# Heads of the two expert stages of a decoder trunk: routing tables on GpSimd, first rows split ahead of the tables, two matrices split beside attention's end

## The chip, the core and the metric

The kernel runs on one core of one Trainium2 chip. The core has five engines with queues of their own: TensorE (PE in the profile; PEld is its weight load), VectorE (DVE), ScalarE (ACT), GpSimd (POOL) and SyncE (SP, which only issues transfers here). The metric is the device time of one launch in microseconds. Lower is better.

## What is computed

A trunk of two layers over 512 tokens of width 1024. Layer 0 mixes tokens with RWKV-7, layer 1 with forgetting attention. After each mixer comes a LayerNorm and a mixture of 16 experts, whose router is shared: the best of four groups, and in it the best two experts.

```python
h = layer_norm(ALPHA * h + mixed, ln_g[i, 0], ln_b[i, 0])
ffn = shared_router_moe(h, router_w, router_bias, ...)
h = layer_norm(ALPHA * h + ffn, ln_g[i, 1], ln_b[i, 1])
...
s = jax.nn.sigmoid(xt @ router_w); s_sel = s + router_bias
grp_score = jnp.sum(lax.top_k(s_sel, 2)[0], -1); g_star = jnp.argmax(grp_score, -1)
_, loc = lax.top_k(in_grp, TOP_K); e_idx = g_star[:, None] * EXPERTS_PER_GROUP + loc
gate = jnp.take_along_axis(s, e_idx, axis=1); gate = gate / jnp.sum(gate, -1, keepdims=True)
...
hid = jax.nn.silu(xb @ w_gate[e]) * (xb @ w_up[e]); ys = hid @ w_down[e]
out = jax.ops.segment_sum(ys * row_gate[:, None], row_tok, num_segments=n_tok + 1)[:n_tok]
```

## The kernel before

All tokens stand in four tiles of 128. Every fp32 product is made of three: both operands are split into a high part (`wh`, `xm`, `xh`; ACT copies to fp32r, line 200 for weights, line 64 for rows) and a low part (the difference, on VectorE, lines 203 and 65), and high by high, low by high and high by low are summed.

An expert's weights are six matrices of 1 MB (`place`): two of gate, two of up, two of down. They go through a ring of eight landing tiles `raw`, numbered m = 0, 1, 2, ... over all experts. `wsplitA(m)` makes the high part on ACT, `wsplitB(m)` the low part on VectorE and then issues the load of matrix m+8 on SP. Six high and six low tiles exist.

`moe` is one expert stage and is called for both layers. Its **head** comes before the loop over experts. On VectorE it picks group and experts (lines 209 to 231, ending in the 0/1 table `selb`), on PE it counts positions, and then it finds the rows of the first expert: `first(0)` makes the list of 128 token rows and gathers them into `xg` (line 253, an indirect transfer on POOL), `gather2(0)` gathers the half rows of the next 64 tokens (second block) into `xo` (line 262), and `first(1)` does the same as `first(0)` for expert 1. What follows on VectorE, in this order: the low part of matrix 0 (`loA(0)`); the routing tables (lines 391 to 408: position and block of each token, the two choices of each token as masks `m1` and `mk`, sums over experts `red`, the index `idx` and the gate `rec`); the gates of expert 0 in three bf16 pieces `gp` (lines 411 to 414); then, after the eight scatters of the tables on POOL have been issued (line 423), the low parts of the gathered rows `xm`, of matrix 1, of the second block's rows `xh`, and of matrices 2 to 5.

The loop over experts begins with `more(0)`, the second block of expert 0, which is run if it has over 128 tokens, as it does in both layers here. On PE that is: products with matrices 0 and 1 (16 of 512 columns), twelve small ones with `gp` that give the block's gates (`gates0(1)`, line 419), products with matrices 2 and 3 (32 of 256 columns), transposes, and products with 4 and 5. PE takes them in this order:

```python
guB(w[0],0); guB(w[1],1); nc.scalar.activation(xo,pgo,AF.Copy)
if e==0: gates0(1)
guB(w[2],2); upB(0,f2)
guB(w[3],3); upB(1,f2); hidBT(0); hidBS(0); hidBT(1); hidBS(1)
```

The work inside `moe` is issued as written. The attention stage `fox` is ordered by `Threads`, a planner in which each strand says what it needs and how long it holds an engine; its last strands are `t_oproj` (output projection, residual sum at line 1254), `t_last` (LayerNorm, `ln_steps`: statistics on VectorE, root and normalisation on ACT, scale and shift as four VectorE operations, line 148) and `t_route` (transposes, router product, sigmoid).

Of the kernel before, what the change touches and what calls it, by code (L numbers as in the profile page):

```python
# [176 lines left out]

def moe(C, L, W, hd, zd, load, tail, late=()):

# [4 lines left out]
    with ExitStack() as ctx:  # L184
# [205 lines left out]
        bl=su[:,256:320].rearrange("p (a b) -> p a b",b=NE); code=su[:,320:384].rearrange("p (a b) -> p a b",b=NE); pos=pp[:,0:NT,:]  # L390
        V.tensor_scalar(bl,pos,127.5,None,op0=ALU.is_gt)
        for n in (255.5,383.5): V.scalar_tensor_tensor(bl,pos,n,bl,op0=ALU.is_gt,op1=ALU.add)
        V.scalar_tensor_tensor(code,pos,64.0,C.e4[:,None,:].to_broadcast([128,NT,NE]),op0=ALU.mult,op1=ALU.add)
        V.scalar_tensor_tensor(code,bl,-8191.0,code,op0=ALU.mult,op1=ALU.add)
        mk=su[:,384:512].rearrange("p (c t e) -> p c t e",c=2,e=NE); m1=mk[:,1].rearrange("p t (g e) -> p (t g) e",g=4)
        V.memset(m1[:,:,0],0.0); V.tensor_copy(m1[:,:,1],selv[:,:,0])
        V.tensor_tensor(m1[:,:,2],selv[:,:,0],selv[:,:,1],op=ALU.add)
        V.tensor_tensor(m1[:,:,3],m1[:,:,2],selv[:,:,2],op=ALU.add)
        V.tensor_tensor(mk[:,1],mk[:,1],sel,op=ALU.mult)
        V.tensor_tensor(mk[:,0],sel,mk[:,1],op=ALU.subtract)  # L400
        mt=sTs[0].rearrange("p a b -> p (a b)").rearrange("p (c t e) -> p c t e",c=2,e=NE); red=p1.tile([128,3,8],F32,name="red"); idx=p1.tile([128,8],I32,name="idx")
        ct=lambda t: t.rearrange("p c t e -> p (c t) e"); bc=lambda t: t[:,None,:,:].to_broadcast([128,2,NT,NE])
        V.tensor_tensor(mt,mk,bc(code),op=ALU.mult)
        V.tensor_reduce(red[:,0,:,None],ct(mt),axis=AX.X,op=ALU.add); V.tensor_copy(idx,red[:,0])
        V.tensor_tensor(mt,mk,bc(s),op=ALU.mult)
        V.tensor_reduce(red[:,1,:,None],ct(mt),axis=AX.X,op=ALU.add)
        V.tensor_tensor(red[:,2,0:4],red[:,1,0:4],red[:,1,4:8],op=ALU.add); V.reciprocal(red[:,2,0:4],red[:,2,0:4]); V.tensor_scalar(red[:,2,0:4],red[:,2,0:4],1.0/ALPHA,None,op0=ALU.mult)
# [953 lines left out]
```

## Time and profile before

| | us |
|---|---|
| median of 3 runs | 1638.11 (1634.1 to 1641.88) |
| profiled execution, own time | 1635.95 |
| its span in the trace | 1634.2 |

| engine | busy us | share |
|---|---|---|
| PE | 1459.5 | 89% |
| PEld | 1192.7 | 73% |
| DVE | 1163.1 | 71% |
| ACT | 919.5 | 56% |
| POOL | 530.7 | 32% |

The span is the stretch between the trace's first and last record; 1.75 us of the execution's own time lie outside it. A timeline row gives start, duration, engine, line, operation, output and inputs with their shapes, and in brackets how long the engine had been idle and what released it. The granted clock is 1.00 where TensorE runs at 2.4 GHz and 0.50 where it runs at 1.2 GHz.

### The profile page before, as it was taken

Reading aid. Unit: us, or ns where it says so; the run is one execution under the profiler, and the core shown is the slowest. Engines: PE = TensorE matmul, PEld = TensorE weight load, DVE = VectorE, ACT = ScalarE, POOL = GpSimd, SP = SyncE. Lnnn points to the kernel's source line nnn. Section 1 sums busy time; section 2 is a strip of 40 time slices with the busy share of each in tenths; the row PEclk is TensorE's granted clock in tenths of the full one; section 3 lists DMA queues with packets and bytes.
Section 4 is the critical chain, followed back from the end, with each engine's and each line's share of the span. In section 5 each row is a group of like instructions: output and inputs, shape, how many; then the busy total and the mean of one; then the engine's idle time right before and its main releaser. Section 6 shows DMA issues by size and latency. Waiting matters only on the chain. (4 is left out here: it accounts for less than half of the span.)

```text
span 1634.2 us, 24892 instructions
## 1 busy us (share of the span) xinstructions
PE 1459.5 (89%) x9125; PEld 1192.7 (73%) x9125; DVE 1163.1 (71%) x1873; ACT 919.5 (56%) x1355; POOL 530.7 (32%) x431
## 2 busy tenths in 40 slices
PE   6998977889976799999999699999885999999992
PEld 2587865887765688888887577777674888888881
DVE  7647779477585796887895637556647786968984
ACT  2553573534334486767885436545424786858872
POOL 4104785413242433322342323101104233313422
PEclk9998998587987899999999799999995999999996
DMA  7325532133345799897992424112427797979962
GB/s 221 123 84 187 162 99 83 27 98 117 111 142 189 239 331 316 287 358 232 357 344 94 157 72 123 37 61 72 155 104 227 244 364 247 358 249 346 350 204 106
DMA packets 202521, 313.61 MB, mean 192 GB/s; under 512 B 27914, under 2 KB 123490, under 8 KB 202356
## 3 DMA queue, kind: packets, MB, share of 16 engines
q1 hardware_dynamic: 178820, 267.74, 48.1%
q0 software_dynamic: 18816, 37.31, 8.0%
q10 hardware_dynamic: 4720, 6.44, 1.1%
q8 instruction: 93, 1.52, 0.4%
q14 instruction: 72, 0.59, 0.1%
HBM read 296.42 MB, written 41.75 MB: 207 GB/s over the span
## 5 line engine op out<-in xcount | busy, mean ns | idle before, releaser
L203 DVE TENSOR_TENSOR wl<-raw,wh 128x2048 fp32r<-128x2048 f32 (+1 forms) x168 | 334.7, 2006 | 5.9 <-DVEq L344 5.9
L200 ACT ACTIVATE wh<-raw 128x2048 fp32r<-128x2048 f32 (+1 forms) x168 | 282.7, 1688 | 15.7 <-ACT wh L200 9.0
L339 POOL DMA_INDIRECT zd<-yt,TB x38 | 113.7, 2992 | 432.2 <-ACT yt L306 386.0
L68 PE MATMUL bank<-wh,xm 128*128 128x256 f32 (+1 forms) x768 | 249.9, 325 | 3.9
L69 PE MATMUL bank<-wl,xm 128*128 128x256 f32 (+1 forms) x768 | 245.1, 319 | 0.0
L70 PE MATMUL bank<-wh,xm 128*128 128x256 f32 (+1 forms) x768 | 244.9, 319 | 0.0
L68 PEld LDWEIGHTS bank<-wh,xm 128*128 128x128 f32 x768 | 144.6, 188 | 26.0 <-issue 14.6
L69 PEld LDWEIGHTS bank<-wl,xm 128*128 128x128 f32 x768 | 144.7, 188 | 11.5
L70 PEld LDWEIGHTS bank<-wh,xm 128*128 128x128 f32 x768 | 144.6, 188 | 11.3
L203 DVE TENSOR_TENSOR wl<-rawo,wh 128x2048 fp32r<-128x2048 f32 (+1 forms) x56 | 110.2, 1980 | 24.9 <-ACT wh L200 24.4
L68 PE MATMUL bank<-wh,wh 128*128 128x512 f32 x256 | 111.5, 436 | 1.4 <-DVE kl L1169 0.8
L68 PE MATMUL bank<-wh,hm 128*128 128x512 f32 x256 | 111.3, 435 | 0.0
L70 PE MATMUL bank<-wh,wl 128*128 128x512 f32 x256 | 101.1, 395 | 3.6 <-DVE wl L1240 3.6
L70 PE MATMUL bank<-wh,hm 128*128 128x512 f32 x256 | 101.1, 395 | 0.0
L69 PE MATMUL bank<-wl,hm 128*128 128x512 f32 x256 | 100.8, 394 | 0.0
L200 ACT ACTIVATE wh<-rawo 128x2048 fp32r<-128x2048 f32 (+1 forms) x56 | 93.4, 1668 | 13.1 <-PE bank L70 9.0
L69 PE MATMUL bank<-wl,wh 128*128 128x512 f32 x256 | 100.6, 393 | 0.0
L1062 POOL TENSOR_TENSOR wl<-raw,wh 128x512 fp32r<-128x512 f32 x29 | 41.2, 1432 | 88.6 <-ACT wh L1061 87.0
L262 POOL DMA_INDIRECT xo<-hd,TB x30 | 61.1, 2037 | 11.9 <-issue 8.6
L64 ACT ACTIVATE xm<-bank 128x512 fp32r<-128x512 f32 x64 | 38.3, 598 | 42.5 <-PE bank L280 38.9
L68 PEld LDWEIGHTS bank<-wh,wh 128*128 128x128 f32 x256 | 49.2, 192 | 15.1 <-issue 6.0
L1197 ACT ACTIVATE sb<-sb,st 128x512 f32<-128x512 f32 (+1 forms) x64 | 35.8, 560 | 43.2 <-DVE st L1193 27.3
(531 smaller groups left out, 3504.1 us busy)
## 6 DMA issues: line engine op xcount, KB each, us to landing
raw<-in_moe_w_gate_dram SPq DMA_DIRECT2D x48, 1024.0 KB
raw<-in_moe_w_up_dram SPq DMA_DIRECT2D x48, 1024.0 KB
raw<-in_moe_w_down_dram SPq DMA_DIRECT2D x48, 1024.0 KB
rawo<-in_moe_w_up_dram SPq DMA_DIRECT2D x16, 1024.0 KB
rawo<-in_moe_w_down_dram SPq DMA_DIRECT2D x16, 1024.0 KB
rawo<-in_moe_w_gate_dram SPq DMA_DIRECT2D x14, 1024.0 KB
raw<-in_fx_w_in_dram SPq DMA_DIRECT2D x12, 1024.0 KB
raw<-in_rw_wk_dram SPq DMA_DIRECT2D x4, 1024.0 KB
```

Source lines behind the costliest of these rows:

```text
L64: nc.scalar.activation(hi,src,AF.Copy)
L68: nc.tensor.matmul(out,ah,bh,start=start,stop=False)
L69: nc.tensor.matmul(out,ah,bl,start=False,stop=False)
L70: nc.tensor.matmul(out,al,bh,start=False,stop=stop)
L200: Q=slice(None) if q is None else QS[q]; nc.scalar.activation(his[m%NH][:,Q],raws[m%NR][:,Q],AF.Copy)
L203: Q=slice(None) if q is None else QS[q]; V.tensor_tensor(los[m%NH][:,Q],raws[m%NR][:,Q],his[m%NH][:,Q].bitcast(F32),op=ALU.subtract)
L262: nc.gpsimd.indirect_dma_start(out=xo,out_offset=None,in_=hd.rearrange("t (h n) -> (t h) n",h=2), in_offset=bass.IndirectOffsetOnAxis(ap=T ...
L339: nc.gpsimd.indirect_dma_start(out=zd[:,:],out_offset=bass.IndirectOffsetOnAxis(ap=ix[0:n],axis=0), in_=y[0:n],in_offset=None,bounds_check ...
L1062: (V if d else G).tensor_tensor(lo[n][:,Q],raw[:,Q],hi[n][:,Q].bitcast(F32),op=ALU.subtract)
L1197: S.activation(SB[u][:,0:N],SB[u][:,0:N],AF.Exp,bias=ST[u][:,0:1],scale=-1.0,accum_out=ST[u][:,1:2])
```

## The change

In both heads, `mk` (the masks of first and second choice) is made from a second threshold `thr1`, by one VectorE comparison and two POOL operations ahead of the first gather. The sums over experts are no longer VectorE reductions; `total` halves the 16 experts in four additions on POOL. The sum for the gates is issued on POOL between `first(0)` and `gather2(0)`, that for the index after the gathers. The VectorE part of the tables shrinks to five small operations and two on `red`. The splitting of the gathered rows and of matrices 1 to 5 is written ahead of the rest of the tables, and the gates `gr`, `gp` of expert 0 come behind the low part of matrix 5.

In layer 1 alone (`pre=2`), the high and low parts of matrices 0 and 1 are made in `fox`, on ACT and VectorE, by a new strand `t_early` and at the end of the last `t_last`; their successors, matrices 8 and 9, are then loaded at the head's start. The last tile's LayerNorm there is `ln_quick`: statistics by halves, and subtraction with scale, then multiplication with shift, as two VectorE operations for each half, with no ACT normalisation.

```diff
+def ln_quick(C, th, z, i, gb, bb, mark, eps=LN_EPS, keys=()):
+    V=C.nc.vector; sm=C.sm[:,i%4]; N=(slice(0,512),slice(512,1024))
+    for n in range(2):
+        yield from th.need(*keys[n:n+1])
+        V.bn_stats(sm[:,6*n:6*n+6],z[:,N[n]]); yield 'V',.69
+    V.bn_aggr(sm[:,12:14],sm[:,0:12].rearrange("p (a b) -> p a b",a=2))
+    V.tensor_scalar(sm[:,14:15],sm[:,13:14],eps,None,op0=ALU.add)
+    C.nc.scalar.activation(sm[:,15:16],sm[:,14:15],AF.Sqrt)
+    sub=lambda n: V.scalar_tensor_tensor(z[:,N[n]],z[:,N[n]],sm[:,12:13],gb[:,N[n]],op0=ALU.subtract,op1=ALU.mult)
+    sub(0); V.reciprocal(sm[:,14:15],sm[:,15:16]); yield 'V',1.2
+    for n in range(2):
+        if n: sub(1)
+        V.scalar_tensor_tensor(z[:,N[n]],z[:,N[n]],sm[:,14:15],bb[:,N[n]],op0=ALU.mult,op1=ALU.add); yield 'V',.69*(n+1)
+        mark(n)
...
-        for m in range(NH): wsplitA(m)
+        for m in range(pre,NH): wsplitA(m)
...
+        V.tensor_tensor(m0,rk,C.thr1[:,None,:].to_broadcast([128,16,4]),op=ALU.is_lt)
+        G.tensor_tensor(m0,m0,gs.rearrange("p t g -> p (t g)")[:,:,None].to_broadcast([128,16,4]),op=ALU.mult)
+        G.tensor_tensor(mk[:,1],selb,mk[:,0],op=ALU.subtract)
...
         first(0)
...
+            for n in (8,4,2): G.tensor_tensor(t[:,:,0:n],t[:,:,0:n],t[:,:,n:2*n],op=ALU.add)
+            G.tensor_tensor(out,t[:,:,0],t[:,:,1],op=ALU.add)
+        G.tensor_tensor(mt2,mk,bc(s),op=ALU.mult); total(red[:,1],mt2)
+        G.tensor_tensor(red[:,2,0:4],red[:,1,0:4],red[:,1,4:8],op=ALU.add)
...
-        loA(0); V.tensor_copy(sel,selb)
+        V.reciprocal(red[:,2,0:4],red[:,2,0:4]); V.tensor_scalar(red[:,2,0:4],red[:,2,0:4],1.0/ALPHA,None,op0=ALU.mult)
+        for m in range(pre): load(m+NR)
...
+        if not pre: loA(0)
+        for hf in range(2): xposeT(xgs[0],hf,tr[hf]); xposeS(hf,tr[hf])
+        if not pre: loA(1)
+        xposeB()
+        for m in range(2,NH): loA(m)
+        G.tensor_tensor(mt,mk,bc(code),op=ALU.mult); total(red[:,0],mt)
+        G.tensor_copy(idx,red[:,0])
...
         V.tensor_tensor(gr,s[:,:,ORDER[0]],red[:,2,0:4],op=ALU.mult)
...
-        for hf in range(2): xposeT(xgs[0],hf,tr[hf]); xposeS(hf,tr[hf])
-        loA(1); xposeB()
-        for m in range(2,NH): loA(m)
...
     def t_last(i):
-        yield from need(f"r{i}0",f"r{i}1")
-        yield from after.norm(i,z[i],th,z[i])
+        if i<NT-1: yield from need(f"r{i}0",f"r{i}1")
+        yield from after.norm(i,z[i],th,z[i],(f"r{i}0",f"r{i}1"))
+        if i==NT-1: after.lo(0,1); after.lo(1)
+    def t_early():
+        yield from need(f"r{NT-1}0")
+        yield .8
+        after.hi(0,0); yield 'S',.95
+        after.lo(0,0); yield 'v',1.15
+        after.hi(0,1); after.hi(1); yield 'S',2.9
...
-        moe(C,1,W,hd[1],zd[1],load[1],0)
+        moe(C,1,W,hd[1],zd[1],load[1],0,pre=2)
```

VectorE's queue in the head of layer 0, before (`gp` are expert 0's gates, `xm` and `xh` the gathered rows, `wl` a matrix's low part):

```order
L411 TENSOR_TENSOR gr<-s,red 128x4
L413 CAST gp<-gr 128x4
L414 TENSOR_TENSOR gr<-gr,gp 128x4
L413 CAST gp<-gr 128x4
L414 TENSOR_TENSOR gr<-gr,gp 128x4
L413 CAST gp<-gr 128x4
L65 TENSOR_TENSOR xm<-bank_3958,xm 128x512
L65 TENSOR_TENSOR xm<-bank_3959,xm 128x512
L203 TENSOR_TENSOR wl_3944<-raw_62,wh_3938 128x2048
L65 TENSOR_TENSOR xh<-bank_3958,xh 128x256 x2
L203 TENSOR_TENSOR wl_3945<-raw_63,wh_3939 128x2048
L203 TENSOR_TENSOR wl_3946<-raw_64,wh_3940 128x2048
```

The same place now, from the low part of matrix 0 on; three more rows of `gr` and `gp` follow the last one:

```order
L219 TENSOR_TENSOR wl_3945<-raw_61,wh_3939 128x2048
L65 TENSOR_TENSOR xm<-bank_3960,xm 128x512
L65 TENSOR_TENSOR xm<-bank_3961,xm 128x512
L219 TENSOR_TENSOR wl_3946<-raw_62,wh_3940 128x2048
L65 TENSOR_TENSOR xh<-bank_3960,xh 128x256 x2
L219 TENSOR_TENSOR wl_3947<-raw_63,wh_3941 128x2048
L219 TENSOR_TENSOR wl_3948<-raw_64,wh_3942 128x2048
L219 TENSOR_TENSOR wl_3949<-raw_65,wh_3943 128x2048
L219 TENSOR_TENSOR wl_3950<-raw_66,wh_3944 128x2048
L437 TENSOR_TENSOR gr<-s,red 128x4
L439 CAST gp<-gr 128x4
L440 TENSOR_TENSOR gr<-gr,gp 128x4
```

The six operations of the gates stood ahead of the rows and are now behind the low parts of matrices 2 to 5 (`wl` from `raw_63` to `raw_66`). PE's queue has kept its order.

POOL's queue in the head of layer 1, before, from the first gather on:

```order
L253 DMA xg_17915<-hd_136,i_17974 128x1024
L262 DMA xo<-hd_136,i_18008 128x512
L253 DMA xg_17916<-hd_136,i_17974 128x1024
L269 TENSOR_LOAD cnt x2
L423 DMA tab_17908<-rec,idx 8192x4 x8
L427 DMA TB<-tab_17908 128x256
L429 DMA TB_17910<-tab_17908 128x1x256
L430 TENSOR_SCALAR TB_17910<-TB_17910,odd 128x64
```

And now:

```order
L274 DMA xg_17922<-hd_138,i_17982 128x1024
L286 TENSOR_TENSOR sT_17921<-su,s 128x128
L284 TENSOR_TENSOR sT_17921<-sT_17921 128x8x8
L284 TENSOR_TENSOR sT_17921<-sT_17921 128x8x4
L284 TENSOR_TENSOR sT_17921<-sT_17921 128x8x2
L285 TENSOR_TENSOR red<-sT_17921 128x8
L287 TENSOR_TENSOR red<-red 128x4
L293 DMA xo<-hd_138,i_18024 128x512
L274 DMA xg_17923<-hd_138,i_17982 128x1024
L300 TENSOR_LOAD cnt x2
L432 TENSOR_TENSOR sT_17920<-su 128x128
L284 TENSOR_TENSOR sT_17920<-sT_17920 128x8x8
```

Six operations for the gates' sum stand between the first gather and that of the second block, and seven for the index (two are shown) ahead of the scatters.

VectorE's queue at the end of attention, before, from the last tile's two residual sums on:

```order
L1254 SCALAR_TENSOR_TENSOR raw_66<-raw_66,bank_3956 128x512
L1254 SCALAR_TENSOR_TENSOR raw_66<-raw_66,bank_3957 128x512
L123 BN_STATS sm<-raw_66 128x6 x2
L124 BN_AGGR sm<-sm 128x2
L125 TENSOR_SCALAR sm<-sm 128x1
L130 RECIPROCAL sm<-sm 128x1
L131 SCALAR_TENSOR_TENSOR sm<-sm 128x1
L148 TENSOR_TENSOR raw_66<-raw_66,raw_63 128x512 x4
L209 TENSOR_TENSOR su<-s,rbt 128x64
```

And now:

```order
L1277 SCALAR_TENSOR_TENSOR raw_66<-raw_66,bank_3958 128x512
L157 BN_STATS sm<-raw_66 128x6
L1337 TENSOR_TENSOR wl_3945<-raw_61,wh_3939 128x1024
L1277 SCALAR_TENSOR_TENSOR raw_66<-raw_66,bank_3959 128x512
L157 BN_STATS sm<-raw_66 128x6
L158 BN_AGGR sm<-sm 128x2
L159 TENSOR_SCALAR sm<-sm 128x1
L161 SCALAR_TENSOR_TENSOR raw_66<-raw_66,sm,raw_63 128x512
L162 RECIPROCAL sm<-sm 128x1
L165 SCALAR_TENSOR_TENSOR raw_66<-raw_66,sm,raw_63 128x512
L161 SCALAR_TENSOR_TENSOR raw_66<-raw_66,sm,raw_63 128x512
L165 SCALAR_TENSOR_TENSOR raw_66<-raw_66,sm,raw_63 128x512
```

One half of a low part of matrix 0 stands between the two residual sums, and the four operations behind the statistics are fused ones.

## Rows read from the trace of the kernel before

**Rows 1.** table by stretch, layer 0 experts: busy by engine, clock, DMA share
```profile
580.00:604.00 24.00, 23.85 (x143) 20.66 (x142) 21.89 (x18) 19.70 (x20) 11.31 (x6) 1.00 1.02 339
```

**Rows 2.** timeline of DVE, layer 0 head: start us, us, line, operation, tiles
```profile
530.54 2.29 DVE L203 TENSOR_TENSOR wl<-raw,wh 128x2048 fp32r<-128x2048 f32 x1
...
537.02 0.15 DVE L411 TENSOR_TENSOR gr<-s,red 128x4 f32<-128x4 f32 x1
...
538.01 0.40 DVE L413 CAST gp<-gr 128x4 bf16<-128x4 f32 x1
...
538.09 1.28 DVE L65 TENSOR_TENSOR xm<-bank,xm 128x512 fp32r<-128x512 f32 x2
...
539.29 2.28 DVE L203 TENSOR_TENSOR wl<-raw,wh 128x2048 fp32r<-128x2048 f32 x1
...
541.49 0.41 DVE L65 TENSOR_TENSOR xh<-bank,xh 128x256 fp32r<-128x256 f32 x1
...
542.71 8.95 DVE L203 TENSOR_TENSOR wl<-raw,wh 128x2048 fp32r<-128x2048 f32 x4
```

**Rows 3.** timeline of PE, layer 0 head, up to hidden rows
```profile
534.15 1.97 PE L280 MATMUL bank<-ident,xg 128*128 128x128 f32 x8 [5.64 <-DMA xg<-hd,i]
...
542.01 0.77 PE L314 MATMUL bank<-wh,xh 128*128 128x512 f32 x1 [2.06 <-issue]
...
547.71 0.45 PE L419 MATMUL bank<-gp,yt 128*128 128x1 bf16 x12
...
548.02 0.37 PE L314 MATMUL bank<-wh,xh 128*128 128x256 f32 x1
...
551.90 0.55 PE L326 MATMUL bank<-pair,xo 128*128 128x64 f32 x4
```

**Rows 4.** timeline of ACT, layer 0 head: the second copy of gathered rows
```profile
536.16 0.60 ACT L64 ACTIVATE xm<-bank 128x512 fp32r<-128x512 f32 x1 [0.20 <-PE bank L280]
```

**Rows 5.** timeline of POOL, layer 0: issue of the first gather
```profile
527.08 1.10 POOL L253 DMA_INDIRECT xg<-hd,i  x1 [4.35 <-issue]
```

**Rows 6.** timeline of DVE, layer 1: LayerNorm of the last tile
```profile
1221.09 1.28 DVE L123 BATCH_NORM_STATS2 sm<-raw 128x6 f32<-128x512 f32 x2
...
1224.31 2.75 DVE L148 TENSOR_TENSOR raw<-raw,raw 128x512 f32<-128x512 f32 x4 [0.88 <-ACT raw L135]
```

**Rows 7.** timeline of PE, layer 1 head
```profile
1225.78 1.11 PE L154 MATMUL bank<-ident,raw 128*128 128x128 f32 x4 [5.33 <-DVE raw L148]
...
1243.67 1.94 PE L280 MATMUL bank<-ident,xg 128*128 128x128 f32 x8 [3.10 <-DMA xo<-hd,i]
...
1253.71 0.76 PE L314 MATMUL bank<-wh,xh 128*128 128x512 f32 x1 [2.11 <-DVE xh L65]
...
1260.17 0.45 PE L419 MATMUL bank<-gp,yt 128*128 128x1 bf16 x12
```

**Rows 8.** timeline of POOL, layer 1: issue of the first two gathers
```profile
1239.10 1.07 POOL L253 DMA_INDIRECT xg<-hd,i  x1 [4.34 <-issue]
1240.48 1.05 POOL L262 DMA_INDIRECT xo<-hd,i  x1 [0.30 <-DVE sg L248]
```

**Rows 9.** costliest groups, the smallest form of POOL: busy us, mean ns
```profile
L717 POOL COPY Lam<-Ep 128x8 f32<-128x8 f32 x8 | 3.6, 445 | 0.5
```

**Rows 10.** timeline of PE, a gap in the RWKV mixer
```profile
477.75 1.11 PE L919 MATMUL rb<-ident,y 128*128 128x128 f32 x4 [5.36 <-DVE y L917]
```

**Rows 11.** table by stretch around that gap and in the layer 1 head
```profile
474.00:476.00 2.00, 0.00 (x0) 0.00 (x0) 2.00 (x3) 0.00 (x0) 1.27 (x1) 0.63 0.00 0
482.00:484.00 2.00, 1.58 (x16) 1.49 (x13) 1.47 (x4) 1.62 (x4) 0.42 (x1) 1.00 0.57 174
1254.00:1258.00 4.00, 4.00 (x10) 3.13 (x10) 3.97 (x3) 0.00 (x1) 3.08 (x4) 0.50 0.95 271
1260.00:1264.00 4.00, 4.00 (x43) 3.83 (x42) 3.88 (x4) 1.88 (x2) 3.61 (x2) 1.00 1.01 393
```

**Rows 12.** timeline of DVE: a LayerNorm addition beside a POOL subtraction
```profile
487.76 1.65 DVE L148 TENSOR_TENSOR res<-res,raw 128x512 f32<-128x512 f32 x1
```

More of the change, by code (lines that the diff above doesn't have):

```diff
@@ L175, in place, with moe @@
     queue.dma_start(raw.rearrange("p (k n) -> p k n",k=kk),(M[:,hf*n:(hf+1)*n] if w==1 else M[hf*128*kk:(hf+1)*128*kk,:]).rearrange("(k p) n -> p k n",p=128))
-def moe(C, L, W, hd, zd, load, tail, late=()):
+def moe(C, L, W, hd, zd, load, tail, late=(), pre=0):
     nc,tc=C.nc,C.tc; V=nc.vector
@@ L256, in moe, with total @@
         first(0)
+        mt=sTs[0].rearrange("p a b -> p (a b)").rearrange("p (c t e) -> p c t e",c=2,e=NE); red=p1.tile([128,3,8],F32,name="red"); idx=p1.tile([128,8],I32,name="idx")
+        mt2=sTs[1].rearrange("p a b -> p (a b)").rearrange("p (c t e) -> p c t e",c=2,e=NE)
+        ct=lambda t: t.rearrange("p c t e -> p (c t) e"); bc=lambda t: t[:,None,:,:].to_broadcast([128,2,NT,NE])
+        def total(out, t):
+            t=ct(t)
+            for n in (8,4,2): G.tensor_tensor(t[:,:,0:n],t[:,:,0:n],t[:,:,n:2*n],op=ALU.add)
+            G.tensor_tensor(out,t[:,:,0],t[:,:,1],op=ALU.add)
+        G.tensor_tensor(mt2,mk,bc(s),op=ALU.mult); total(red[:,1],mt2)
+        G.tensor_tensor(red[:,2,0:4],red[:,1,0:4],red[:,1,4:8],op=ALU.add)
         oh2=ys[1][:,256:512].bitcast(BF16).rearrange("p (t n) -> p t n",t=NT); rows(2,0,oh2,C.slots2); i2=p1.tile([128,1],I32,name="i2")
@@ L271, in moe @@
         most=p1.tile([1,1],I32,name="most"); V.tensor_reduce(most,cnt,axis=AX.X,op=ALU.max)
-        loA(0); V.tensor_copy(sel,selb)
+        bl=su[:,256:320].rearrange("p (a b) -> p a b",b=NE); code=su[:,320:384].rearrange("p (a b) -> p a b",b=NE); pos=pp[:,0:NT,:]
+        V.tensor_scalar(bl,pos,127.5,None,op0=ALU.is_gt)
+        for n in (255.5,383.5): V.scalar_tensor_tensor(bl,pos,n,bl,op0=ALU.is_gt,op1=ALU.add)
+        V.scalar_tensor_tensor(code,pos,64.0,C.e4[:,None,:].to_broadcast([128,NT,NE]),op0=ALU.mult,op1=ALU.add)
+        V.scalar_tensor_tensor(code,bl,-8191.0,code,op0=ALU.mult,op1=ALU.add)
+        V.reciprocal(red[:,2,0:4],red[:,2,0:4]); V.tensor_scalar(red[:,2,0:4],red[:,2,0:4],1.0/ALPHA,None,op0=ALU.mult)
+        for m in range(pre): load(m+NR)
         Xm=fx("xm",[128,2,KT,128],F32R); Xh=fx("xh",[128,KT,64,2],F32R)
@@ L387, in rest @@
             scatter(ix,ys[0],128)
[L390 to L407, printed above, removed]
@@ L1014, in fox_vload @@
     C.nc.sync.dma_start(k4(dst),P['win'][k*512:(k+1)*512,2048+n*512:2048+(n+1)*512].rearrange("(k p) n -> p k n",p=128))
-FX_SCHED=(0,.5,-1,0,0,2,4,6,15)+(0,)*16
+FX_SCHED=(0,.5,-1,0,0,2,4,6,15)+(0,)*17
 def fox(C, comb, P, after):
@@ L1265, in fox @@
     for i in range(NT): th.add(t_tokens(i))
-    for g,bi in zip((t_values(0),t_wv(),t_gates(),t_values(1),t_weights(),t_qk(),t_post(0),t_post(1),t_score(),t_soft(),t_norm(),t_transpose(),t_av(),t_oparts(),t_oproj(0),t_oproj(1),*[t_last(i) for i in range(NT)],t_route()),
-                    (*bias,*[0]*8)): th.add(g,bi)
+    for g,bi in zip((t_values(0),t_wv(),t_gates(),t_values(1),t_weights(),t_qk(),t_post(0),t_post(1),t_score(),t_soft(),t_norm(),t_transpose(),t_av(),t_oparts(),t_oproj(0),t_oproj(1),*[t_last(i) for i in range(NT)],t_early(),t_route()),
+                    (*bias,*[0]*9)): th.add(g,bi)
     th.run()
@@ L1275, in free, with norm @@
     def free(s, n): s.load(n)
-    def norm(s, i, z, th, out):
-        yield from ln_steps(s.C,th,z,i,out,s.gb,s.bb,lambda n: th.done.add(f"y{i}{n}"))
+    def norm(s, i, z, th, out, keys=()):
+        mark=lambda n: th.done.add(f"y{i}{n}")
+        if i==NT-1 and z is out: yield from ln_quick(s.C,th,z,i,s.gb,s.bb,mark,keys=keys)
+        else: yield from ln_steps(s.C,th,z,i,out,s.gb,s.bb,mark)
         (s.C.nc.sync if i==NT-1 else s.C.nc.gpsimd).dma_start(s.hd[i*128:(i+1)*128,:],out)
@@ L1298, in free, with hi, lo @@
         else: s.load(n)
+    def hi(s, m, q=None):
+        Q=slice(None) if q is None else slice(q*1024,(q+1)*1024); s.C.nc.scalar.activation(s.C.his[m][:,Q],s.C.raws[m][:,Q],AF.Copy)
+    def lo(s, m, q=None):
+        Q=slice(None) if q is None else slice(q*1024,(q+1)*1024); s.C.nc.vector.tensor_tensor(s.C.los[m][:,Q],s.C.raws[m][:,Q],s.C.his[m][:,Q].bitcast(F32),op=ALU.subtract)
     def logits(s, i, hT, pl):
```

5 lines of the change are left out of this document (3 added, 2 removed).

## Prediction

> **What bounds the kernel now.** I read the table by stretch first, then the timelines of the two heads engine by engine. Inside the loops over experts TensorE is busy 23.85 of 24 us at full clock [rows 1]: no transfer and no split holds it there. So whatever time one head gains or loses for TensorE reaches the end, and no later wait takes it up. I count every part of the change by when TensorE gets past `more(0)` in that head.
>
> In the heads TensorE waits. In layer 0 the first rows land and are transposed at 534.15 [rows 3], ACT's second copy of them ends at 536.76 [rows 4], but VectorE reaches their low part only at 538.09 and those of the second block at 541.49 [rows 2], since the tables lie in between. TensorE starts the second block at 542.01, issues `gates0(1)` at 547.71, the products with matrices 2 and 3 at 548.02, and is through with them at 551.90 [rows 3]. In that stretch it did not wait: `gp` had been ready since 538.41, and VectorE finished matrix 5 at 551.66, just ahead of its next use [rows 2]. Layer 1 repeats this: rows at 1243.67, second block at 1253.71, `gates0(1)` at 1260.17 [rows 7].
>
> **Layer 0, step by step.** (1) The rows. Without the tables VectorE can take the first half's low part at about 536.0 and the second's when ACT's copy ends at 536.76; 0.69 later, at 537.45, it is free for matrix 1. Before that stood at 539.29 [rows 2]. Everything behind it, the second block's rows included, comes 1.85 us earlier. The low part of matrix 0 now follows the short tables: it would end near 534.4 and stays hidden behind the landing at 534.15 and ACT's copies.
>
> (2) The gates. Here the change adds a wait. `gp` now stands behind the low parts of matrices 2 to 5, 8.95 us [rows 2], and its own six operations last 1.4 (537.02 to 538.41). The four low parts start at 542.71 - 1.85 = 540.86 and end at 549.8; `gp` is ready at 551.2. TensorE gets through matrices 0 and 1 at 547.71 - 1.85 = 545.9 and then stands at `gates0(1)`, with all other products of the block queued behind it. ACT and POOL stand behind these: the block's scatter and the two gathers after it, which have half an expert of slack. `gates0(1)` runs at 551.2 instead of 547.71, **3.5 us later**. That VectorE has more than twice the work of TensorE between the two points is why the order matters: before, the gates cost nothing because they were taken while TensorE had no rows yet.
>
> (3) The clock. A gap of 5.3 us is new there. After a gap of 5.36 us in the mixer [rows 10] the clock had fallen within it (0.63 over 474 to 476) and was at 1.00 in the stretch from 482 on [rows 11], at most 4.3 us after the restart at 477.75. In layer 1's head TensorE ran at 0.50 from 1254 to 1258 and at 1.00 from 1260 [rows 11], 4.3 to 6.3 us after it began at 1253.71. So I take the products behind the gates to start at 1.2 GHz and to stay there for 4.2 us; half of that is lost, **2.1 us**. The bounds are 0, if the clock stays, and 3.1, half of 6.3; I take the value nearest to the row that has a gap of the same length.
>
> Layer 0 together: +3.5 + 2.1 = **+5.6 us**.
>
> **Layer 1.** (4) The last LayerNorm. Before, statistics began at 1221.09 and the first transposes at 1225.78 [rows 6, 7]. Now half the statistics are done beforehand (-0.64), and subtraction with scale (0.69, the price of one of the four operations in [rows 6], beside the root on ACT) and multiplication with shift (0.69) replace the two small steps, ACT's normalisation and two of the four: the first half is ready near 1223.8, **1.9 us** earlier. The three ACT operations of `t_early` (1.05, 1.05 and 1.9) must fit between the last transposed copy, which ends at 1217.97, and the root, near 1222.2; they end at 1222.0. If the first were late, up to 1.9 us would go back, so the bounds of this term are 0 and -1.9. The half low part between the residual sums (1.2 us) lies in idle time of VectorE, and the rest of matrices 0 and 1 (3.4 us) lies behind the LayerNorm, where VectorE waits for the sigmoid longer than that.
>
> (5) The gathers. The first goes out 1.9 us earlier, at 1237.2. Before, 4.57 us passed from issue to transposes (1239.10 to 1243.67) [rows 7, 8]; in layer 0, where five weight loads are in flight, it took 7.07 (527.08 to 534.15) [rows 3, 5]. Now the loads of matrices 8 and 9 are issued on SP behind the table's store, much earlier than before, and lie beside the gather. Bounds 4.57 and 7.07; I take 5.2, near the low end, because two of the five loads are under way and the DMA is otherwise idle: rows at 1242.4. Between the two gathers POOL has six new operations. The smallest one that the trace shows takes 0.445 [rows 9], so with one of 128 elements about 2.5 us (nothing below 0 is possible here, and 3.5 is the upper end). The second gather goes from 1240.48 to about 1240.9 and its rows land near 1245. VectorE has nothing else to do: low parts of the rows until 1245.7, second block from 1247.1 instead of 1253.71, **6.6 us earlier**.
>
> (6) The gates again. Low parts of the second block's rows end at 1247.9, those of matrices 2 to 5 at 1256.9, `gp` at 1258.3. TensorE has been waiting since about 1253.5. `gates0(1)` runs at 1258.3 instead of 1260.17: of 6.6 us, **1.9 remain**, and the clock of step 3 takes 2.1. Layer 1 together: **+0.2 us**.
>
> **Small ones.** The comparison for `mk` stands where VectorE waits for PE's counts anyway: nothing. Scatters of the tables start some 1 to 3 us earlier; nobody waits for them on the path, since the block's own scatter waits for its output. Removed VectorE work (some 20 small operations) lay in the stretch already counted.
>
> **Sum.** +5.6 + 0.2 = +5.8 on the profiled execution's 1635.95, hence 1641.7. That execution lies 2.2 below the median of the three runs, 1638.11; put on the median the forecast is **1643.8 us**, 0.35% more. A measurement of this kernel can tell about 0.5%, or 8.2 us, from no change. So I expect a small loss that counts as the same.
>
> **Rivals.**
> - *The clock stays up* in both gaps. For: the gap is only 5 us, and in layer 0 the half speed lasts until shortly before it. Against: [rows 10, 11]. It gives +5.8 - 4.2 = +1.6, 1639.7. Chance 0.13.
> - *Late rows, slower.* Place: the gathers of layer 1 beside loads 8 and 9, and the second block's gather behind POOL's six operations in both heads. At layer 0's 7.07 us the first rows come 1.9 us later than I took; with 3.5 us on POOL instead of 2.5 the second gather is 1 us later in each head, and in layer 0 the DMA is full. It decides from the point where the second block's rows land after 538.2 in layer 0 or after 1245.4 in layer 1. Price 1 + 1.9 = 2.9 or more, +8.7, 1646.8. For: layer 0's row; against: fewer loads in layer 1. Chance 0.18.
> - *POOL holds VectorE up.* An addition that takes 0.69 alone [rows 6] took 1.65 beside a POOL subtraction [rows 12]. If the seven operations for the index, 3.1 us at 0.445 each, ran beside the low parts that decide, VectorE would be up to 3.1 us later in each head: +5.8 + 6.2 = +12.0, 1650.1. Against: they follow right behind the gathers and are over before matrices 2 to 5 begin. Chance 0.03. The Trainium skill (GPSIMD Engine Reference, Key points) says that the two engines share their SBUF interfaces, with contention where a VectorE instruction has two SBUF inputs, and that elementwise work is about twice as fast on VectorE; both speak against this change, and the trace agrees with the first (0.69 and 1.65).
> - *The gates do not hold TensorE*, so that only the earlier rows count: -1.85 and -6.6, so -8.5, 1629.6. For: the low parts of matrices 2 and 3 are early enough. Against: both queues as listed, each in order. Chance 0.06.
> - The forecast itself has 0.60.
>
> **How the numbers follow.** The forecast's own bounds (clock to 3.1 in each gap, rows by 1 us either way) are 1642.5 to 1647, and medians of three runs scatter by about 2. With the clock rival below and late rows above, 8 in 10 lie between 1636.5 and 1650. Slower by over 0.5% (over 1646.3): two thirds of late rows, all of POOL's hold and a tenth of the forecast, 0.12 + 0.03 + 0.06 = 0.21. Faster by over 0.5% (under 1629.9): the last rival, 0.06. The same: 0.73.
>
> **What would show it.** In the profile after, VectorE's low parts of the rows should come straight behind ACT's copies; TensorE should start the second block near 540.2 and 1247; the longest new wait of TensorE should be the product with `gp` behind VectorE's last `gp` operation, 4 to 5.5 us in each head; and the products with matrices 2 and 3 should take over 5.5 us instead of 3.9 (548.02 to 551.90), at 0.50. Wrong would be: no wait before `gates0(1)`; the clock at 1.00 behind it; rows landing after 1244; or a root on ACT that waits for the weight copies.

## Result and profile after

The changed kernel takes **1648.17 us** (median of 12 runs, 1642.97 to 1656.13) against 1634.36 for the kernel before on the same chip (12 runs): ratio **1.0079, interval 1.0061 to 1.0097**. It is slower by 13.8 us. The forecast was +5.8 and "the same"; the time lies within the range, near its upper end, and the loss is more than twice what was forecast. Part of that is luck. The range stood on a median of three runs, 1638.11; twelve runs of the kernel before give 1634.36, and put on that the range ends near 1646, below the measured time. By the prediction's own line of 0.5% the outcome is "slower", to which it gave 0.21, not "the same", 0.73.

The profiled execution took 1647.53 (span 1645.8, before 1634.2). I cut both spans at the same instructions. A *head* runs from the selection (`selb`, line 231 before, 247 after) to ACT's first copy of expert 0's output (`yt<-bank`).

| stretch, us | before | again | after | again | after - before |
|---|---|---|---|---|---|
| start to layer 0's selection | 523.81 | 523.39 | 520.25 | 524.78 | -3.56 |
| layer 0's head | 52.68 | 52.67 | 59.33 | 59.28 | **+6.65** |
| other experts of layer 0 | 313.28 | 313.41 | 313.45 | 313.59 | +0.17 |
| to layer 1's selection | 346.10 | 345.85 | 347.05 | 347.07 | +0.95 |
| layer 1's head | 52.99 | 53.05 | 59.32 | 59.21 | **+6.33** |
| other experts of layer 1 | 313.17 | 313.33 | 313.54 | 313.55 | +0.37 |
| to the end | 32.2 | 32.2 | 32.9 | 32.4 | +0.7 |

The "again" columns are second traces, from the experiments. The heads repeat within 0.1 us, so their 13.0 us are the change's. The first stretch has the same code in both kernels and spreads by 4.5 us in two traces of the changed one.

**Layer 0's head.** The timeline of PE after, which answers to [rows 3]:

```profile
536.50 0.76 PE L351 MATMUL bank<-wh,xh 128*128 128x512 f32 x1 [2.26 <-issue]
...
546.42 0.16 PE L445 MATMUL bank<-gp,yt 128*128 128x1 bf16 x1 [3.26 <-DVE gp L439]
546.99 0.16 PE L445 MATMUL bank<-gp,yt 128*128 128x1 bf16 x1 [0.41 <-DVE gp L439]
547.39 0.41 PE L445 MATMUL bank<-gp,yt 128*128 128x1 bf16 x10 [0.24 <-DVE gp L439]
547.66 0.56 PE L351 MATMUL bank<-wh,xh 128*128 128x256 f32 x1
...
553.77 0.55 PE L363 MATMUL bank<-pair,xo 128*128 128x64 f32 x4
...
557.47 0.50 PE L351 MATMUL bank<-wh,hs 128*128 128x512 f32 x1 [1.80 <-DVE hs L65]
```

The second block starts 16.25 us after the selection (18.20 before), but then TensorE waits three times for `gp`. The timeline of DVE after, which answers to [rows 2], shows why: the gates' pieces follow the low parts.

```profile
537.20 8.89 DVE L219 TENSOR_TENSOR wl<-raw,wh 128x2048 fp32r<-128x2048 f32 x4
546.01 0.16 DVE L437 TENSOR_TENSOR gr<-s,red 128x4 f32<-128x4 f32 x1
...
547.17 0.17 DVE L439 CAST gp<-gr 128x4 bf16<-128x4 f32 x1
```

Behind the gap the products with matrices 2 and 3 take 6.11 us (547.66 to 553.77) instead of 3.88. The tables by stretch have the granted clock third from the end of each row: of before,

```profile
548.00:551.90 3.90, 3.90 (x39) 3.90 (x36) 3.79 (x4) 1.78 (x2) 3.29 (x3) 1.00 1.03 402
```

and of after, for the same products in layer 0 and in layer 1:

```profile
547.60:553.80 6.20, 6.20 (x41) 6.20 (x39) 0.64 (x2) 0.00 (x0) 1.60 (x2) 0.59 0.82 306
1267.10:1273.60 6.50, 6.50 (x40) 6.50 (x38) 0.64 (x2) 0.00 (x0) 1.23 (x2) 0.56 0.84 305
```

The last term I had not seen. In the timeline of ACT after, the table load for the second block's silu waits for TensorE:

```profile
554.85 1.28 ACT L365 ACT_TABLE_LOAD   x1 [11.05 <-PE bank L363]
556.14 0.28 ACT L365 ACTIVATE sT<-bank 128x128 f32<-128x128 f32 x1
```

Before, it ran at 548.52, right behind ACT's copy of `xo`, while TensorE was busy; there the silu's ACTIVATE waited itself. ACT before:

```profile
548.52 1.28 ACT L328 ACT_TABLE_LOAD   x1
553.07 0.28 ACT L328 ACTIVATE sT<-bank 128x128 f32<-128x128 f32 x1 [3.27 <-PE bank L326]
```

From the end of the products to `dnB` (the products of the hidden rows `hs` with matrices 4 and 5) it was 2.49 us (551.90 to 554.39), now 3.70. PE before:

```profile
554.39 0.50 PE L314 MATMUL bank<-wh,hs 128*128 128x512 f32 x1 [0.46 <-DVE hs L65]
```

In layer 1 it was 2.36 and is 3.68.

**Layer 1's head.** PE after, answering to [rows 7]:

```profile
1247.51 1.94 PE L317 MATMUL bank<-ident,xg 128*128 128x128 f32 x8 [2.35 <-DMA xg<-hd,i]
1253.91 1.09 PE L347 MATMUL bank<-ident,xo 128*128 128x128 f32 x4 [4.46 <-DMA xo<-hd,i]
1256.03 0.76 PE L351 MATMUL bank<-wh,xh 128*128 128x512 f32 x1 [1.04 <-DVE xh L65]
...
1265.91 0.16 PE L445 MATMUL bank<-gp,yt 128*128 128x1 bf16 x1 [4.46 <-DVE gp L439]
...
1266.88 0.40 PE L445 MATMUL bank<-gp,yt 128*128 128x1 bf16 x10 [0.24 <-DVE gp L439]
1267.15 0.56 PE L351 MATMUL bank<-wh,xh 128*128 128x256 f32 x1
```

The second block's rows are used 7.39 us after their gather's issue (1246.52 to 1253.91) and land after 7.2 (4.1 before). In the timeline of POOL, answering to [rows 8], the gather goes out behind six small operations; in the queue of SP two loads of 1 MB go out around it, the first 0.21 us ahead, after 7.6 us in which SP waited for the counts:

```profile
1242.82 1.11 POOL L274 DMA_INDIRECT xg<-hd,i  x1 [1.62 <-DVE yt L269]
1243.96 0.47 POOL L286 TENSOR_TENSOR sT<-su,s 128x128 f32<-128x128 f32 x1
...
1245.81 0.20 POOL L287 TENSOR_TENSOR red<-red 128x4 f32<-128x4 f32 x1
1246.52 1.07 POOL L293 DMA_INDIRECT xo<-hd,i  x1 [0.51 <-issue]
```

```profile
SPq L300 <- DVE cnt L297: 7.6, 1, 7.6
...
1246.31 1.01 SPq L191 DMA_DIRECT2D raw<-in_moe_w_up_dram  x2
```

**The last LayerNorm**, DVE and PE after, answering to [rows 6, 7]: from the last residual sum to the first transposes it is 3.43 us, before 5.29 (1220.49 to 1225.78).

```profile
1226.46 0.69 DVE L1277 SCALAR_TENSOR_TENSOR raw<-raw,bank 128x512 f32<-128x512 f32 x1 [0.32 <-PE bank L70]
```

```profile
1229.89 1.11 PE L170 MATMUL bank<-ident,raw 128*128 128x128 f32 x4 [3.46 <-DVE raw L165]
```

### The profile page after: what moved, and what is told of

It is laid out like the page before. It is cut to its first block, busy times and chain, and to the rows that moved or that the text cites. A ratio compares the mean times of both kernels' runs of the same rounds, so it can differ in the third digit from the quotient of the medians.

```text
span 1645.8 us, 24893 instructions
## 1 busy us (share of the span) xinstructions
PE 1458.5 (89%) x9125; PEld 1191.6 (72%) x9125; DVE 1162.3 (71%) x1848; ACT 918.1 (56%) x1354; POOL 539.2 (33%) x461
## 5 line engine op out<-in xcount | busy, mean ns | idle before, releaser
L219 DVE TENSOR_TENSOR wl<-raw,wh 128x2048 fp32r<-128x2048 f32 (+1 forms) x166 | 329.9, 2002 | 5.6 <-DVEq L381 5.6
L216 ACT ACTIVATE wh<-raw 128x2048 fp32r<-128x2048 f32 (+1 forms) x166 | 279.1, 1685 | 18.9 <-ACT wh L216 9.0
L70 PEld LDWEIGHTS bank<-wh,xm 128*128 128x128 f32 x768 | 144.6, 188 | 11.4
```

Of the source, the lines that this page charges most:

```text
L70: nc.tensor.matmul(out,al,bh,start=False,stop=stop)
L219: Q=slice(None) if q is None else QS[q]; V.tensor_tensor(los[m%NH][:,Q],raws[m%NR][:,Q],his[m%NH][:,Q].bitcast(F32),op=ALU.subtract)
```

## Experiments

Theory A: the gates' wait, with the clock that falls in it, is most of the loss; part D of it: the table load behind TensorE adds 1.2 us in each head. Theory B: layer 1's late rows are most of it. Theory C: POOL's work slows VectorE, or the loss has no place. Heads are given as layer 0 / layer 1, against 52.7 / 53.0 in before and 59.3 / 59.3 in the changed kernel. Each ratio is against runs of the kernel before taken beside it (medians of 1634.0 to 1635.9 us).

### 1. Gates early, on the changed kernel

```diff
         xposeB()
+        g0=...; gp=...; gr=...   (the block of gr and gp, from behind the tables)
         for m in range(2,NH): loA(m)
```

> The changed kernel, with the three pieces of the gates (gr, gp) made ahead of the low parts of matrices 2 to 5 instead of behind them. Theory A (TensorE waits for gp behind four low parts, and its clock falls in that gap): in both heads the wait of 3.3 to 4.5 us ahead of the gate products goes, and the products with matrices 2 and 3 take 3.9 to 4.2 us again instead of 6.1 and 6.4; layer 0 gives back 3.2+2.2=5.4 us, layer 1 about 4.5+2.2=6.7, together about 12 of the 13.8 us lost: 1636 us, ratio to the kernel before 0.999 to 1.003. Theory B (the loss is the late second rows of layer 1, and the gates only fill time that another wait would take): the low part of matrix 2 or the rows take the gap over, at most 3 us come back, ratio 1.005 to 1.008. Theory C (GpSimd's added work slows VectorE, or the loss has no single place): no change within 1 us, ratio 1.006 to 1.010.

1640.53 us, ratio **1.0022** (1.0003 to 1.0041); heads 54.77 / 53.88, so 10.0 of the 13.0 us come back. The gates run without a wait and the products behind them take 3.88 us (546.83 to 550.71):

```profile
546.52 0.45 PE L445 MATMUL bank<-gp,yt 128*128 128x1 bf16 x12
546.83 0.37 PE L351 MATMUL bank<-wh,xh 128*128 128x256 f32 x1
...
550.71 0.56 PE L363 MATMUL bank<-pair,xo 128*128 128x64 f32 x4
```

A holds, B and C fall as main causes: neither the late rows (still 4.05 us of wait in layer 1) nor POOL's work was touched. It gave back 2 us less than A said: the clock now falls later, in `dnB`, which costs 1.5 us in each head (section on the hardware).

### 2. Gates late, on the kernel before

```diff
-        g0=...; gp=...; gr=...   (ahead of the rows)
         loA(1); xposeB()
         for m in range(2,NH): loA(m)
+        g0=...; gp=...; gr=...
```

> The kernel before, with the gates' pieces made behind the low parts of matrices 2 to 5, and nothing else: the reverse of the experiment with early gates. Theory A: the rows' low parts come 1.3 us earlier, the gates' pieces end where the low parts end now (551.6 and 1263.3 us), TensorE waits 4 to 5 us for them behind the products with matrices 0 and 1, and the second block's last products start 3 us (clock as before) to 6 us (clock falls in the gap) later in each head: together 6 to 12 us, ratio 1.004 to 1.0075. Theories B and C (the place of the gates does not decide): within 1.5 us, ratio 0.999 to 1.001.

1647.36 us, ratio **1.0081** (1.0056 to 1.0106), the same loss as the whole change and a little over A's range; heads 59.11 / 57.65.

```profile
551.70 0.16 PE L414 MATMUL bank<-gp,yt 128*128 128x1 bf16 x1 [4.59 <-DVE gp L432]
...
552.67 0.41 PE L414 MATMUL bank<-gp,yt 128*128 128x1 bf16 x10 [0.24 <-DVE gp L432]
```

Six operations of VectorE, 1.4 us in all, cost 6.4 and 4.7 us by their place alone, with no table on POOL and no new LayerNorm.

### 3. Loads 8 and 9 later, on the changed kernel

```diff
-        for m in range(pre): load(m+NR)            (SyncE, behind the counts)
         xposeB()
+        for m in range(pre): load(m+NR,nc.scalar)
```

> The changed kernel, with layer 1's loads of matrices 8 and 9 issued by ScalarE behind its copies of the second block's rows instead of by SyncE behind the counts, so that they no longer run beside the second gather. Both theories: the rows land 4 to 5 us after the gather's issue instead of 7.4. Theory A: VectorE's work behind them, the gates' pieces at its end, moves up by the same 2.5 to 3 us and no more, the wait of TensorE for gp of 4.5 us stays: about 1645.5 us, ratio 1.005 to 1.008. Theory B: with the rows in time most of layer 1's loss of 6.3 us goes, and with it more than half of the whole: ratio 1.002 to 1.005. Theory C: nothing, ratio 1.006 to 1.010.

1645.23 us, ratio **1.0060** (1.0032 to 1.0088); heads 60.01 / 55.68. PE in layer 1:

```profile
1257.62 1.09 PE L346 MATMUL bank<-ident,xo 128*128 128x128 f32 x4 [0.81 <-DMA xo<-hd,i]
1269.62 0.16 PE L445 MATMUL bank<-gp,yt 128*128 128x1 bf16 x1 [4.10 <-DVE gp L439]
```

The rows are in time (9.83 us after the selection instead of 13.83), and TensorE then waits 4.10 us for `gp` as before. Layer 1's head gains 3.6, over half of its 6.3, and layer 0's nothing; another 1.5 went to the clock, which falls in layer 1's `dnB` here (23.67 us from `dnB` to the first output instead of 22.14). So the loads did delay the gather, and of both heads' 13.0 us that is the smaller part: A.

### 4. Scratch of its own for POOL, on the changed kernel

```diff
-        mt=sTs[0].rearrange(...)
+        mt=p1.tile([128,2,NT,NE],F32,name="mt")
-        mt2=sTs[1].rearrange(...)
+        mt2=mt
```

> The changed kernel, with a tile of their own for GpSimd's sums of the tables, which lay in the two tiles of the second block's silu. Theory A with its part D (the silu, which now waits for GpSimd too, hands its wait for TensorE to the table load of 1.28 us ahead of it): the table load runs ahead of TensorE's end again, the second block's last products start 1.2 us earlier in each head, about 2.4 us in all: ratio 1.005 to 1.0075. Without D the table load stays behind TensorE, or its 1.28 us are covered by another wait: no change, ratio 1.006 to 1.010.

1642.82 us, ratio **1.0040** (1.0023 to 1.0057), just under A's range; heads 57.04 / 56.23, 2.3 and 3.1 us shorter. ACT in layer 0:

```profile
551.53 1.28 ACT L365 ACT_TABLE_LOAD   x1
562.55 0.28 ACT L365 ACTIVATE sT<-bank 128x128 f32<-128x128 f32 x1 [9.73 <-PE bank L363]
```

D holds: without POOL as a second writer of the silu's tiles the ACTIVATE waits for PE itself, and the load runs ahead. From the end of the products to `dnB` it is 2.36 us in both heads, 1.3 less. The rest is not shown to be the edit's: the rows came 0.2 and 0.6 us earlier, and the clock came back earlier (5.4 and 5.3 us for the products of matrices 2 and 3 instead of 6.1 and 6.4), as it did in layer 1 of the changed kernel's second trace (5.2). The table load's 1.28 us is the Trainium skill's 1283 ns for one (ScalarE activation tables: per-element evaluation and per-set limits, What a function is on this engine); the trace agrees.

### 5. The three edits together

> The three edits together: gates' pieces early, loads 8 and 9 late, scratch of their own. Theory A: 5.4+1.2 us in layer 0 and 6.7+1.2 and some 2.5 of the late rows in layer 1 come back, in all 15 to 17 us, against 13.8 lost, so the last LayerNorm's 1.75 us is what is left as a gain, with the rows ahead of it: 1631 to 1634 us, ratio 0.997 to 1.000. Theory B or C: half of the loss or more stays, ratio 1.003 or above.

1630.83 us, ratio **0.9978** (0.9959 to 0.9996), now faster than before; heads 53.45 / 49.06. Both heads together give back 16.1 us; the three edits alone gave 10.0, 3.0 and 5.4, so their shares overlap. The changed kernel's idea works in layer 1, whose head is 3.9 us shorter than in before. Layer 0 gains nothing: its products with matrices 2 and 3 end 2.06 us earlier after the selection than in before (26.04 instead of 28.10), but TensorE then takes longer to `dnB` (3.73 us instead of 2.49), and in `dnB` the clock falls (23.68 us to the first output instead of 22.10). One suspect is that the second block's rows stand behind the low part of matrix 1 on VectorE; experiment 6 tests it. PE's row and the table by stretch:

```profile
538.76 0.76 PE L350 MATMUL bank<-wh,xh 128*128 128x512 f32 x1 [2.26 <-issue]
```

```profile
549.50:552.40 2.90, 1.55 (x12) 1.42 (x12) 1.75 (x7) 0.82 (x3) 1.09 (x1) 1.00 0.96 303
552.40:556.00 3.60, 3.54 (x10) 2.85 (x11) 0.53 (x3) 0.31 (x1) 0.21 (x1) 0.63 1.01 387
```

### 6. Second rows first in layer 0, on the kernel of 5

```diff
-        if not pre: loA(1)
         xposeB()
+        if not pre: loA(1)
```

> The kernel with the three edits, and in layer 0 the second block's rows transposed and split ahead of the low part of matrix 1. Its trace showed VectorE splitting those rows 1.7 us late, behind that low part (2.28 us), and TensorE idle for 2.26 us there. Theory A: the second block's first products start 1.5 to 2 us earlier in layer 0, the low part of matrix 1 is done ahead of its use (TensorE needs some 3.4 us for matrix 0 at half clock), and the head of layer 0 is 28 us instead of 29.8; layer 1 is as it was, 25.4. Ratio 0.995 to 0.999. A rival: the low parts are then the bound (five of 2.23 us behind the rows), the product with matrix 1 waits for its own, and the head stays at 29 to 30 us.

1632.05 us, ratio **0.9982** (0.9967 to 0.9996); heads 54.35 / 49.05. A miss: the block starts 1.2 us earlier, and TensorE stands later for VectorE's multiplication with the gates (`su`), which comes only behind four low parts. The rival holds in its cause, the low parts as the bound, but not in its place: the product with matrix 1 does not wait, and `dnB` starts 30.67 us after the selection, not 29 to 30.

```profile
541.21 8.92 DVE L219 TENSOR_TENSOR wl<-raw,wh 128x2048 fp32r<-128x2048 f32 x4
...
550.31 0.88 DVE L358 TENSOR_SCALAR su<-bank,g 128x256 f32<-128x256 f32 x2
```

```profile
550.85 0.66 PE L362 MATMUL bank<-pair,su 128*128 128x64 f32 x4 [2.63 <-DVE su L358]
```

### 7. Gates in VectorE's idle time, on the kernel of 6

The block of `gr` and `gp` moves up, behind the two operations on `red[:,2,0:4]` and ahead of the rows.

> The kernel with the three edits and the second rows first in layer 0, with the gates' pieces made before the rows are split, where VectorE stood idle for 1.31 us in layer 0 (533 us in that trace) and 1.09 us in layer 1, instead of between the rows and the low parts. Theory A with its correction (once the gates are early, the chain is VectorE's own queue: low parts 2 to 5 and, behind them, the products with the gates, for which TensorE waits 2.6 us in layer 0 and 1.1 in layer 1): the low parts end 1.0 to 1.3 us earlier in both heads, the head is 29.4 to 29.8 us in layer 0 (30.67 without the move) and 24.4 to 25 in layer 1 (25.39); ratio 0.996 to 0.999. A rival: the pieces delay the rows by their own 1.2 us, or the clock takes back what is won: the heads as they were within 0.3, ratio as it was, 0.997 to 1.000.

**1627.50 us**, ratio **0.9959** (0.9941 to 0.9976), the lowest of all, though its interval overlaps those of 5 and 6; heads 54.24 / 47.80, together only 0.5 us shorter than in 5. In layer 0 `dnB` starts 1.0 us earlier after the selection (29.70 instead of 30.67), as expected, and the clock takes it back: 24.54 us from there to the first output instead of 23.68.

Layer 1 gains 1.25 us, but not in the expected way. VectorE is through with its low parts only 0.54 us earlier, and `dnB` starts 0.3 us later (25.69 instead of 25.39). The gates' pieces hold up the low parts of the first rows, as the rival had it, and the second block starts 0.6 us later; its products with matrices 0 and 1 then take 6.57 us instead of 5.51, longer at half clock. TensorE so came late enough to find VectorE's multiplication done, and the stop that it had in 6 is gone. That stop, in PE of 6:

```profile
1260.31 0.66 PE L362 MATMUL bank<-pair,su 128*128 128x64 f32 x4 [1.14 <-DVE su L358]
```

In 7 the clock stayed up in `dnB`, 22.11 us to the first output instead of 23.66. The tables by stretch of 6 and of 7:

```profile
1262.30:1266.00 3.70, 3.68 (x10) 2.92 (x11) 0.49 (x2) 0.31 (x1) 0.82 (x1) 0.58 1.05 396
```

```profile
1264.30:1268.00 3.70, 3.68 (x16) 3.02 (x17) 0.49 (x2) 0.85 (x2) 0.00 (x0) 1.00 1.06 388
```

So this gain is the clock's, and in part luck.

### 8. The LayerNorm alone, on the kernel before

> The kernel before, with the last tile's LayerNorm on VectorE in place of VectorE and GpSimd, and nothing else (no early halves of matrices 0 and 1). Theory A: the stretch from the last residual sum to layer 1's selection is 1.5 to 2 us shorter than in before and no wait takes its place; the two heads are as before, 30.6 and 30.9 us within 0.5; the stretch from layer 0's last expert to layer 1's selection is 344.3 us if the ends of layer 0 do not spread, 345 to 346.5 if they do. A rival: VectorE's longer share delays the rows, the heads or the low parts of the first matrices, and the head of layer 1 is 1 us or more longer.

1632.38 us in one run; heads 52.65 / 52.55. From the last residual sum to the selection it is 13.62 us (1219.25 to 1232.87; before 15.38), so 1.76 are gained, as in the changed kernel (13.62). Yet the whole stretch from layer 0's last expert is 346.01, hardly shorter: attention ahead of that sum took 332.39 us, in before 330.72 and 330.48. Experiment 2, whose code for attention is that of before, took 331.79, so this is not the LayerNorm's; it differs between kernels that differ elsewhere, and why is open.

### 9. Both kernels a second time

> The kernel before, unchanged, for a second trace. It tells which differences between traces are none of the change's: the stretch from the start to layer 0's selection (520.25 to 528.91 us in the traces so far, in code that is the same), and the stretch from layer 0's last expert to layer 1's selection, which is 346.10 us in the first trace of before and 347.05 to 347.57 in five traces with the change's attention code, though the last LayerNorm there is 1.75 us shorter. Theory V (that is spread): 346 to 348.5 us here, with the wait for the last scatter 7.4 to 8.7 us. Theory S (the change lengthens layer 0's end by about 1.3 us and attention by 1 to 1.5 more): 346.1 within 0.3, the wait for the last scatter 7.35 within 0.2. The two heads are 30.6 and 30.9 us from selection to the second block's last products, within 0.5, in both.

> The changed kernel, unchanged, for a second trace: what of its difference from before repeats. If the traces of one program repeat as before's two did (within 0.4 us in each stretch): the start to layer 0's selection 520.3 us, the two heads 37.2 and 37.2, the wait behind layer 0's last scatter 8.7 with a packet of instructions fetched some 6.5 us behind its issue, the stretch to layer 1's selection 347.1. If these spread from run to run instead: 520 to 529 us for the first stretch, and the fetch there in one trace and not in the other.

1635.69 and 1651.60 us. Of before every stretch repeats within 0.4 us. Of the changed kernel the heads do as a whole; the start does not (524.78), so it is no part of the difference. Layer 1's head does not repeat in its parts: `dnB` starts 35.5 us after the selection, not 37.2. The products with matrices 2 and 3 take 5.20 us instead of 6.43, and the clock then falls in `dnB`, which takes 23.67 us to the first output instead of 22.14. That the sums agree within 0.1 us is partly chance. The longer wait at layer 0's end repeats too (last section). The table by stretch of the second trace, in `dnB` of layer 1:

```profile
1280.20:1284.00 3.80, 3.74 (x10) 2.97 (x11) 0.49 (x3) 0.31 (x1) 0.00 (x0) 0.62 0.00 0
```

## Why the prediction was right and wrong

- **Step 1, rows 1.85 us earlier:** measured 1.95 (18.20 to 16.25 after the selection). Right.
- **Step 2, `gates0(1)` +3.5 us:** measured +3.24 (23.90 to 27.14). Right, and experiments 1 and 2 show it from both sides.
- **Step 3, clock +2.1 in each head:** measured +2.23 and +2.54. Right; the rival that the clock stays up fell. Where in the head the clock is lost is less sure: in layer 1 of the second trace 1.3 us of it lie in these products and 1.6 in `dnB`.
- **Missing term:** the table load behind TensorE, +1.21 in layer 0 and +1.32 in layer 1, 2.5 in all. The change makes POOL a second writer of the silu's tiles; I took these operations as free of consequences for ACT. With it layer 0 is 3.24 + 2.23 + 1.21 = 6.7, measured +6.65.
- **Step 4, LayerNorm -1.9:** measured 1.86 less from the last sum to the transposes. Right for this place, but the time does not show it: the stretch around it is 0.95 longer. About 1.3 us of that are lost at layer 0's end (last section) and 1.4 in attention ahead of the sum, which experiment 8 leaves open. The forecast had neither.
- **Step 5 failed.** I wrote that loads 8 and 9 are issued behind the table's store, "much earlier than before", and charged them to the first gather. They stood behind SP's reading of the counts and went out at 1246.31, on the second gather, whose rows landed after 7.2 us, not 4.1. The first gather took 4.69 (5.2 forecast) and POOL's six operations 2.05 (2.5). From the selection the second block starts only 1.89 us earlier (17.84 to 15.95), where steps 4 and 5 had given 4.7. This is the late-rows rival's mechanism, at its point (the rows 13.83 us after the selection, where its 1245.4 is 11.4), beside the forecast's and not in its place.
- **Step 6 follows from it:** `gates0(1)` comes 2.50 us later after the selection, not at the same time, and with clock and table load layer 1's head is +6.33. Forecast +0.2 with the LayerNorm, it is +4.6.
- **The sum:** the heads were forecast at +7.7 (5.6 and 2.1) and measured at +13.0. Of the 5.3 between, the table load is 2.5, the gates 2.2 (late in layer 1) and the clock 0.6. The direction was forecast rightly, the size with 5.8 of 13.8 us.
- **Slips in the working:** 1638.11 + 5.8 is 1643.9, not 1643.8. VectorE's 10.3 us between the two points of step 2 are 1.8 times TensorE's 5.7, not more than twice. POOL has shorter operations in the trace of before than 0.445 (a MEMSET of 0.20, last section), and the six took 0.20 to 0.47 each.
- **POOL holds VectorE up:** no. Beside VectorE's low part of matrix 0, POOL's multiplication of 128x128 took 2.19 us (0.46 alone in layer 1, both below); the low part took 2.29, as in before [rows 2]. POOL paid, off the path. That the two contend is what the Trainium skill has (GPSIMD Engine Reference, Key points), and the trace agrees.

VectorE and POOL in the kernel of experiment 5, layer 0, and POOL in the changed kernel, layer 1:

```profile
531.11 2.29 DVE L219 TENSOR_TENSOR wl<-raw,wh 128x2048 fp32r<-128x2048 f32 x1
```

```profile
531.52 2.19 POOL L437 TENSOR_TENSOR mt<-su 128x128 f32<-128x128 f32 x1
```

```profile
1248.94 0.46 POOL L432 TENSOR_TENSOR sT<-su 128x128 f32<-128x128 f32 x1
```

## What to carry to other kernels

When rows come earlier, ask what stood between them and the next use: a few small operations moved behind long ones in an in-order queue cost here more than everything that the move had saved. Scratch borrowed from another engine's tile adds a wait to that engine, and a wait can land on the instruction ahead of the one that needs it. The time at which a queue issues a load follows from everything ahead of it there, register reads included; read it from the queue's own waits, not from the line's place in the code.

## What the runs showed of the hardware

**The clock falls without a long gap, too.** In experiment 5 TensorE stood twice in layer 0 between the products and `dnB`, for 1.16 and 0.46 us, after some 9 us at full clock, and inside `dnB` the granted clock fell to half (0.63 over 552.40 to 556.00, above). From `dnB` to the first output it is 23.68 us instead of 22.1, so 1.6 us of the gain went back; experiment 1 shows the same in both layers (23.64 and 23.65). In before a stop of 0.46 alone cost nothing, and in the changed kernel one of 1.80, soon after the clock had risen, left it at 1.00. Over all twelve traces: in the eleven heads with at most 2.9 us from the end of the products to `dnB` the clock stayed up in `dnB` (22.1 us to the first output); of the thirteen with 3.6 or more it stayed up in three, in which it had come back late (6.1 to 6.4 us for the products with matrices 2 and 3), and the other ten took 23.6 us or more. Which stop brings the fall is not settled.

**An instruction fetch at layer 0's end.** In all eight traces with the changed expert stage POOL goes on 8.2 to 8.7 us after the last scatter's issue, in the four with the old one (before twice, experiments 2 and 8) after 7.0 to 7.4. POOL in before and after:

```profile
890.84 1.60 POOL L339 DMA_INDIRECT zd<-yt,TB  x1 [13.65 <-ACT yt L306]
898.19 0.20 POOL L1034 MEMSET mneg<- 128x128 bf16 x1 [5.75 <-DMA zd<-yt,TB]
```

```profile
894.10 1.60 POOL L376 DMA_INDIRECT zd<-yt,TB  x1 [13.64 <-ACT yt L343]
902.77 0.20 POOL L1057 MEMSET mneg<- 128x128 bf16 x1 [7.06 <-DMA zd<-yt,TB]
```

In the eight a packet of instructions is fetched 6 to 7 us after the scatter's issue (DMA queues of after, 899.3 to 902.8), where the four others have none:

```profile
q14 instruction: 1, 0.01, 0.6%
```

The loads of `zd` then go out 8.16 us after the scatter instead of 6.85. The scatter's own landing, which the rows name, explains little of it: it came 4.99 us behind the issue in after, and 4.60 to 4.79 in three of the four others. This place is a branch past the code for large blocks. The Trainium skill (Runtime: NRT & Kernel Launch, Instruction fetch mechanics) says that a taken branch to a page that isn't held waits for a fetch; the packet fits that, at about 1.3 us. That the change's longer code moved the target is argued, not shown.
